# Two hybrid-attention blocks on one core: the second block's low weight parts on VectorE alone

## Chip, cores and metric

The kernel runs on one core of one Trainium2 chip. The metric is device time in microseconds, the median of several runs. A profile is one execution of the program, taken by the hardware profiler; times within it are microseconds from its first instruction (us), single instructions also nanoseconds (ns).

## What is computed

Two transformer blocks run one after the other on 256 tokens of width 1024, all in float32. The first ends in a mixture of 16,384 single-row experts. The change lies in the second block, which projects its normalised input with one large matrix `w_in` and feeds two mixers:

```python
def second_block(x, p, w_in, ...):
    u = rms_norm(h, norm_pre_mix[i])
    proj = u @ w_in[i]
    hq, hf, hi, hg, nq, nkv, ngate, ga, gb = jnp.split(proj, SPLIT_POINTS, axis=-1)
    kc, vc, ks, vs, kw, vw = jnp.split(nkv, 6, axis=-1)
    y_a = hgrn2_mixer(hq, hf, hi, hg, lower_bounds[i], hg_gnorm[i])
    y_b = nsa_mixer(nq, kc, vc, ks, vs, kw, vw, ngate, cmp_pe_k[i], cmp_pe_v[i], ...)
    merged = (jax.nn.sigmoid(ga) * (y_a @ w_branch_a[i])
              + jax.nn.sigmoid(gb) * (y_b @ w_branch_b[i]))
    h = h + rms_norm(merged @ w_out[i], norm_post_mix[i])
    ...
```

`nsa_mixer` is an attention of 16 query heads over 4 key groups with three branches: keys and values compressed from windows of 32 tokens by a small MLP, selected blocks (at 256 tokens, all of them), and a sliding window. Queries and keys are rotated (rope), and the branches are mixed by sigmoid gates. `hgrn2_mixer` is a gated linear recurrence that takes hq, hf, hi and hg.

## The kernel before, in words

**Split products.** Every weight matrix comes from HBM in blocks of 128x1024 floats, in a fixed list (`_plan`), through a ring of three buffers (w_raw), by DMAs of the SP queue. TensorE multiplies in a rounded format (fp32r), so each block is split: ScalarE writes the rounded part w_hi, and the low part w_lo = w_raw - w_hi is one subtraction of two 128x1024 operands. A product is three matmuls, w_hi by the activations' high part hh, w_lo by hh, w_hi by their low part hl (`mm3`). On PE, rows named ga are products with 512 columns (keys, values, queries, hi), rows named gc those with 256 (the gates' w2_ng, and hq and hf, one block per head).

**Who makes w_lo.** `low_part` (lines 366 to 378) chooses the engine when the program is written, by the planner's own estimates of when GpSimd (POOL) and VectorE (DVE) would be free:

```python
there = self.done["w", self.low][0] + HOP
by = lambda e, t: max(self.busy[e], there) + t
engine = self.nc.gpsimd if by("pool", 2.3) < by("dve", 1.14) + self.offload else self.nc.vector
```

`offload` is the last of four numbers that a stage sets: (depth, margin, backlog, offload). SIDE_A (line 30) holds from `nsa_in` on, for the second block's keys and values and the first half of the queries; SIDE_B (line 31) from the end of `nsa_in` on, for the compressed values, the products hq and hf, the second half of the queries, hi and the heads; SIDE_C (line 32) from `merge` on. The larger offload is, the more often POOL is chosen.

**The order of the work.** The order on PE, VectorE, ScalarE and SP is the order in which the Python code writes instructions. Main products are written in the plan's order. Between them `pump` writes steps of side generators (`turn` for keys and queries, `hidden`, `cmp_scores`, `cmp_values`, `head`) when, by the planner's estimates, what they need is ready ahead of PE, and stops when VectorE or ScalarE is booked more than `backlog` us ahead of PE. So where a low part is booked also moves side steps. A few places wait without choice (`until`): for R, the tokens' scale, for `flat`, the input of the compressing MLP, and for RT, R as a row.

**Names.** kvd, x2t: the keys and values to compress and their transposes. R, diag, RT: the scales, as a diagonal matrix and as a row. kr, krh, krl, krt: rotated keys, their two parts and transposes. qr, ro, qs, qst: queries, rope terms, their split parts and transposes. hid, hidk, hidv, kc, vc: the compressing MLP (weights cw1_k, cw1_v) and its second products. s, nm, nz, nP, nPt, no: a head's scores, negated maximum, normaliser, probabilities, their transposes and the product with the values. sc, pc, pct: the same of the compressed branch. zr, hq, hf: gate products scaled by RT and finished. The stage behind (`merge`) begins with the products hA of the recurrence, whose results are masked with lev, and the products of w2_hg; its constants npm, pmlp, gn and lev are loaded by DMAs of the POOL queue into space that the heads' tiles leave.

Of the kernel before, what the change touches and what calls it, by code (L numbers as in the profile page):

```python
# [26 lines left out]


SIDE_1 = 3, 0.4, 2.5, -9
SIDE_A = 4, 0.4, 2.5, 0  # L30
SIDE_B = 4, 0.3, 3.5, 2
SIDE_C = 4, 0.4, 6, -9
HOP = 0.18
E = mybir.EngineType
# [152 lines left out]
class Feed:  # L187
# [17 lines left out]
    def next(self):  # L205
        self.fetch()
        w = self.blocks[self.used]
        if self.timed:
            self.net.done[self.net.who()] = self.net.done["feed", self.used]
        self.used += 1  # L210
        return w
# [56 lines left out]
class Net:  # L268
# [1109 lines left out]
    def nsa_in(self, pool, lead):  # L1378
# [31 lines left out]
        self.gt = pool.tile([128, 2, 3, 16], F32, name="gt")  # L1410
        self.depth, self.margin, self.backlog, self.offload = SIDE_A

# [73 lines left out]
        def compress(k):  # L1486
            self.until(("flat", k))
            hp = self.acc("hid")[:, :256]
            for c4 in range(4):
                wh, wl = self.block("cw1_" + k, c4)  # L1490
                for s in range(4):
                    c = 4 * c4 + s
                    w = slice(s * 256, s * 256 + 256)
                    if c == 15:
                        nc.tensor.matmul(hp[:64], flat[k][:, c, 0], wl[:, w], start=False, stop=False)
                    nc.tensor.matmul(hp, flat[k][:, c].rearrange("p s m -> p (s m)"), wh[:, w], start=c == 0, stop=c == 15)
                    if c < 15:
                        nc.tensor.matmul(hp[:64], flat[k][:, c, 0], wl[:, w], start=False, stop=False)
                if c4 == 3:
                    self.late.append(lambda: self.side(hidden(k, hp), first=True))  # L1500
                yield
# [58 lines left out]
        self.queries(pool, 0, between=lambda: next(ck))  # L1560
        self.depth, self.margin, self.backlog, self.offload = SIDE_B
        return compress("v")
# [440 lines left out]
```

## Time and profile before

| | us |
|---|---|
| median of three runs (lowest, highest) | 1555.44 (1548.98, 1556.6) |
| the profiled execution's own time | 1553.87 |
| its span, first to last instruction | 1551.0 |
| PE busy in the span | 1363.1 (88%) |
| VectorE busy | 1036.8 (67%) |
| ScalarE busy | 714.8 (46%) |
| GpSimd busy | 395.7 (26%) |
| mean granted TensorE clock | 0.963 of full speed |

The first block with its gathered experts takes the first 898 us or so. The keys, queries and heads of the second block lie from about 905 to 1146.5 us, the recurrence and the merging products follow, and from about 1320 us on the MLP. Busy times overlap between engines; idle time of an engine costs only where others wait for it. A wait is put down to the work that ended it.

### The profile page before, as it was taken

How to read it: one execution, taken by the hardware profiler on the slowest of the kernel's cores; microseconds unless marked ns; L12 is line 12 of the kernel's file. 1: busy time of each engine (PE TensorE's matmuls, PEld its weight loads, DVE VectorE, ACT ScalarE, POOL GpSimd, SP SyncE). 2: the span in 40 equal slices, each digit the busy share in tenths (PEclk: the TensorE clock that was granted, in tenths of full speed). 3: DMA queues.
4: the chain of work that ended last, by engine and by line, in shares of the span. 5: the costliest groups of instructions: out<-in, count | busy, mean ns of one | idle time of the engine just before them, and what ended most of it. 6: DMA issues, size and time to landing. Idle time of an engine off the chain costs nothing.

```text
span 1551.0 us, 18352 instructions
## 1 busy us (share of the span) xinstructions
PE 1363.1 (88%) x5930; PEld 914.3 (59%) x5930; DVE 1036.8 (67%) x2175; ACT 714.8 (46%) x1668; POOL 395.7 (26%) x380
## 2 busy tenths in 40 slices
PE   7999988898878788778787889799999999999996
PEld 3778774444422233222222267778788887999875
DVE  5656767877676677666644567867648666876454
ACT  2434354554444444444433365455643654544443
POOL 2101044333333343333333222533330100000000
PEclk9989989999999999999999999899999999999998
DMA  8756639999999999999999845422254355656553
GB/s 341 249 156 226 193 123 418 421 421 422 421 422 422 421 421 422 421 421 421 421 422 420 342 130 170 142 86 69 82 164 123 111 185 167 185 186 182 189 164 107
DMA packets 81647, 418.99 MB, mean 270 GB/s; under 512 B 10288, under 2 KB 12752, under 8 KB 48656
## 3 DMA queue, kind: packets, MB, share of 16 engines
q0 software_dynamic: 42528, 288.17, 45.5%
q1 hardware_dynamic: 38736, 129.39, 26.1%
q8 instruction: 47, 0.77, 0.2%
q14 instruction: 48, 0.39, 0.1%
q10 hardware_dynamic: 288, 0.27, 0.0%
HBM read 416.75 MB, written 1.05 MB: 269 GB/s over the span
## 4 chain that ended last, share of the span: by engine, by line
PE 42%; DMA 34%; DVE 10%; issue 6%; ACT 3%; POOL 1%; SPq 0%; DVEq 0%; POOLq 0%; ACTq 0%
DMA uv<-in_uv,ids 32%; PE ga L224 19%; PE gc L224 10%; DVE junk L224 2%; PE va L224 2%; PE hA L224 2%; PE s L224 2%; PE wo L224 1%; PE no L224 1%; POOL uv L1164 1%; DVE w_lo L224 1%; PE nPt L224 1%; DMA w_ada<-in_ada 1%; PE o L224 1%; ACT w_hi L224 1%
## 5 line engine op out<-in xcount | busy, mean ns | idle before, releaser
L224 PE MATMUL va<-uv,diag 128*128 128x512 f32 x1024 | 506.9, 624 | 119.8 <-ACT diag L224 118.9
L224 DVE SCALAR_TENSOR_TENSOR junk<-uv,xr 128x1024 f32<-128x1024 f32 x256 | 311.9, 1218 | 203.0 <-DMA uv<-in_uv,ids 195.8
L224 PEld LDWEIGHTS va<-uv,diag 128*128 128x128 f32 x1024 | 179.5, 193 | 412.3 <-ACT diag L224 271.5
L1164 POOL DMA_INDIRECT uv<-in_uv,ids x256 | 247.9, 968 | 399.4 <-PE va L224 260.1
L224 ACT ACTIVATE w_hi<-w_raw 128x1024 fp32r<-128x1024 f32 x215 | 227.4, 1059 | 215.9 <-PE ga L224 139.6
L224 DVE TENSOR_TENSOR w_lo<-w_raw,w_hi 128x1024 fp32r<-128x1024 f32 x172 | 209.9, 1223 | 142.9 <-ACT w_hi L224 142.2
L224 ACT ACTIVATE ga<-dots 128x1 f32<-128x1 f32 x256 | 51.9, 203 | 347.8 <-DVE junk L224 346.6
L224 PE MATMUL gc<-hh,w_hi 128*128 128x256 f32 x520 | 170.6, 328 | 0.0
L224 PE MATMUL gc<-hl,w_hi 128*128 128x256 f32 x520 | 151.8, 292 | 1.4 <-DVE hl L224 1.4
L224 PE MATMUL gc<-hh,w_lo 128*128 128x256 f32 x520 | 151.6, 291 | 1.0 <-POOL w_lo L224 0.7
L224 POOL TENSOR_TENSOR w_lo<-w_raw,w_hi 128x1024 fp32r<-128x1024 f32 x43 | 103.5, 2413 | 169.6 <-ACT w_hi L224 162.4
L224 PEld LDWEIGHTS gc<-hl,w_hi 128*128 128x128 f32 x520 | 104.4, 201 | 11.5 <-issue 9.6
L224 PEld LDWEIGHTS gc<-hh,w_hi 128*128 128x128 f32 x520 | 104.5, 201 | 9.7 <-issue 9.6
L224 ACT ACTIVATE diag<-ident,c 128x128 f32<-128x128 f32 x256 | 102.8, 401 | 8.4
L224 PEld LDWEIGHTS gc<-hh,w_lo 128*128 128x128 f32 x520 | 104.1, 200 | 1.6 <-POOL w_lo L224 1.1
L224 PE MATMUL ga<-w_hi,hh 128*128 128x512 f32 x240 | 99.2, 413 | 0.4 <-ACT hh L224 0.2
L224 PE MATMUL ga<-w_lo,hh 128*128 128x512 f32 x240 | 94.5, 394 | 2.5 <-DVE w_lo L224 2.1
L224 PE MATMUL ga<-w_hi,hl 128*128 128x512 f32 x240 | 94.5, 394 | 0.4 <-DVE hl L224 0.4
L224 ACT ACTIVATE c<-ga,g 128x1 f32<-128x1 f32 x256 | 75.4, 294 | 8.3
L224 POOL TENSOR_TENSOR gr<-gv,nhalf 128x1 f32<-128x1 f32 x8 | 5.2, 656 | 287.8 <-DVE gv L224 287.8
L224 PEld LDWEIGHTS ga<-w_lo,hh 128*128 128x128 f32 x240 | 45.6, 190 | 11.5 <-DVE w_lo L224 3.1
L224 PEld LDWEIGHTS ga<-w_hi,hl 128*128 128x128 f32 x240 | 45.2, 188 | 11.2 <-DVE hl L224 1.3
(408 smaller groups left out, 2147.7 us busy)
## 6 DMA issues: line engine op xcount, KB each, us to landing
w_ada<-in_ada POOLq DMA_DIRECT2D x32, 512.0 KB, 4.7
w_raw<-in_w_up SPq DMA_DIRECT2D x32, 512.0 KB, 3.5
w_raw<-in_w_down SPq DMA_DIRECT2D x32, 512.0 KB, 3.5
ring<-in_ada SPq DMA_DIRECT2D x16, 512.0 KB, 9.6
w_raw<-in_wq SPq DMA_DIRECT2D x16, 512.0 KB, 6.2
w_raw<-in_w_kv SPq DMA_DIRECT2D x12, 512.0 KB, 4.7
w_raw<-in_w_out SPq DMA_DIRECT2D x8, 512.0 KB, 4.7
uv<-in_uv,ids POOLq DMA_INDIRECT x256, 17.7
```

Source lines behind the costliest of these rows:

```text
L224: r = call(out, *args, **kwargs)
L1164: tc.nc.gpsimd.indirect_dma_start(rows[i], None, I["uv"], bass.IndirectOffsetOnAxis(ap=ids[:, i % 16:i % 16 + 1], axis=0))
```

## The change

The offload of SIDE_A and of SIDE_B becomes -99, so that `low_part` never finds POOL earlier than VectorE while these two stages last. Nothing else is edited.

```diff
 SIDE_1 = 3, 0.4, 2.5, -9
-SIDE_A = 4, 0.4, 2.5, 0
-SIDE_B = 4, 0.3, 3.5, 2
+SIDE_A = 4, 0.4, 2.5, -99
+SIDE_B = 4, 0.3, 3.5, -99
 SIDE_C = 4, 0.4, 6, -9
```

In the recorded program 38 subtractions of 128x1024 move from POOL's queue to VectorE's. GpSimd's queue at the point where they stood (the rows named rstd are the small powers behind the norms, DMA rows load the constants of the stage behind):

```order
 L224 TENSOR_TENSOR rstd_6601<-ms_6599,nhalf 128x1
-L224 TENSOR_TENSOR w_lo<-w_raw,w_hi 128x1024
 L224 TENSOR_TENSOR rstd_6646<-ms_6644,nhalf 128x1
 L224 TENSOR_TENSOR rstd_6659<-ms_6657,nhalf 128x1
-L224 TENSOR_TENSOR w_lo<-w_raw,w_hi 128x1024 x35
 L224 DMA npm<-in_n_post_mix 128x1024
 L224 DMA pmlp<-in_n_pre_mlp 128x8
 L224 DMA gn<-in_gnorm 128x1
 L224 DMA lev<-in_lev 128x1024
-L224 TENSOR_TENSOR w_lo<-w_raw,w_hi 128x1024 x2
```

All 38 are gone there, and the four DMAs have nothing in front of them but rstd. VectorE at the beginning of the stage, where the keys to compress are scaled and R is made a diagonal:

```order
 L224 TENSOR_SCALAR Rh<-R 128x1
 L224 TENSOR_SCALAR kvd<-ga,R 128x1024
+L224 TENSOR_TENSOR w_lo<-w_raw,w_hi 128x1024
 L224 TENSOR_SCALAR diag<-ident,R 128x128 x2
 L224 TENSOR_TENSOR w_lo<-w_raw,w_hi 128x1024
 L224 COPY RT<-RT 128x128 x2
-L224 TENSOR_TENSOR w_lo<-w_raw,w_hi 128x1024
+L224 TENSOR_TENSOR w_lo<-w_raw,w_hi 128x1024 x2
```

One more low part stands between kvd and diag, one more behind RT. VectorE in the first gate products, where the MLP's hidk and the first query parts qs are made:

```order
 L224 TENSOR_TENSOR hidk<-hidk,hx 128x128
 L224 SCALAR_TENSOR_TENSOR hidk<-hidk,hx 128x128
+L224 TENSOR_TENSOR w_lo<-w_raw,w_hi 128x1024 x2
+L224 TENSOR_TENSOR zr<-gc,RT 128x256
+L224 TENSOR_SCALAR hidk<-hidk 128x128
+L224 TENSOR_TENSOR hidk<-hidk,hx 128x128
 L224 CAST qs<-qr 128x8x64
 L224 TENSOR_TENSOR qs<-qr,qs 128x8x64
-L224 TENSOR_TENSOR zr<-gc,RT 128x256
-L224 TENSOR_SCALAR hidk<-hidk 128x128
-L224 TENSOR_TENSOR hidk<-hidk,hx 128x128
```

Two low parts stand inside the MLP's chain now, and its end and a gate product come ahead of qs. On PE the side steps move against the main products as VectorE's bookings do: the last head's no products stood 54 ga matmuls ahead of the first hA, and now stand 18 ahead of it. The SP queue, and so the order of all weight loads, is the same.

## Rows read from the trace of the kernel before

**Rows 1.** By stage: length, busy time per engine (instructions), clock, DMA share, GB/s.
```profile
905.00:949.40 44.40, 38.03 (x186) 31.32 (x185) 32.07 (x56) 30.03 (x44) 12.25 (x8) 0.96 0.51 160
949.40:1011.00 61.60, 53.09 (x336) 48.16 (x335) 47.86 (x80) 30.85 (x50) 28.77 (x12) 0.89 0.52 155
1011.00:1057.00 46.00, 42.99 (x264) 34.89 (x264) 29.02 (x88) 28.49 (x91) 15.25 (x7) 0.93 0.25 80
1057.00:1101.00 44.00, 38.64 (x267) 34.30 (x266) 34.93 (x86) 22.32 (x65) 15.80 (x7) 0.88 0.24 75
1101.00:1146.50 45.50, 45.46 (x256) 36.54 (x255) 18.01 (x49) 28.44 (x71) 23.70 (x13) 1.00 0.44 137
1146.50:1242.00 95.50, 95.50 (x581) 84.53 (x580) 72.98 (x167) 42.35 (x85) 4.18 (x6) 1.00 0.39 121
```

**Rows 2.** What PE waited for, 905 to 1146.5: us in total, times, longest.
```profile
PE qst L224 <- DVE qs L224: 3.8, 2, 2.6
PE vc L224 <- issue: 3.0, 1, 3.0
PE nPt L224 <- DVE nP L224: 2.7, 2, 1.9
PE krt L224 <- DVE krh L224: 2.5, 2, 2.0
...
PE RT L224 <- DVE diag L224: 2.2, 1, 2.2
...
PE gc L224 <- POOL w_lo L224: 0.7, 2, 0.4
```

**Rows 3.** All engines in order of time: start, duration, operation [idle before <- what ended it].
```profile
980.72 4.76 POOL L224 TENSOR_TENSOR w_lo<-w_raw,w_hi 128x1024 fp32r<-128x1024 f32 x2 [2.96 <-ACT w_hi L224]
...
980.92 2.34 DVE L224 TENSOR_TENSOR hidk<-hidk,hx 128x128 f32<-128x128 f32 x1
...
983.36 1.09 PE L224 MATMUL kc<-hidk,w2k 128*128 128x64 f32 x4 [1.52 <-issue]
...
986.84 4.86 POOL L224 TENSOR_TENSOR w_lo<-w_raw,w_hi 128x1024 fp32r<-128x1024 f32 x2 [1.36 <-ACT w_hi L224]
...
989.53 2.71 DVE L224 TENSOR_TENSOR qs<-qr,qs 128x512 fp32r<-128x512 f32 x1
...
992.30 0.66 PE L224 MATMUL qst<-ident,qs 128*128 128x128 f32 x4 [2.62 <-DVE qs L224]
```

**Rows 4.** VectorE by tile: count, ns shortest/median/longest, first and last start.
```profile
L224 DVE TENSOR_TENSOR qs<-qr,qs x4: 693/693/2710, 979.7 to 1070.4; 128x512 fp32r<-128x512 f32 x4
...
L224 DVE SCALAR_TENSOR_TENSOR hq<-hq,zr x8: 411/1692/2427, 977.8 to 1103.8; 128x256 f32<-128x256 f32 x8
```

**Rows 5.** By shape, 905 to 1146.5: count | busy us, mean ns | idle before.
```profile
L224 DVE TENSOR_TENSOR w_lo<-w_raw,w_hi 128x1024 fp32r<-128x1024 f32 x15 | 18.3, 1222 | 30.1 <-ACT w_hi L224 29.7 <-PE krt L224 0.5
...
L224 POOL TENSOR_TENSOR w_lo<-w_raw,w_hi 128x1024 fp32r<-128x1024 f32 x38 | 91.4, 2411 | 139.4 <-ACT w_hi L224 132.3 <-PE s L224 3.8 <-PE nPt L224 3.3
```

**Rows 6.** By shape, the stage behind, 1146.5 to 1242.
```profile
L224 DVE TENSOR_TENSOR w_lo<-w_raw,w_hi 128x1024 fp32r<-128x1024 f32 x22 | 26.9, 1222 | 13.2 <-ACT w_hi L224 13.2
```

**Rows 7.** VectorE in order of time, first and last of 23 long entries.
```profile
913.67 1.60 DVE L224 TENSOR_TENSOR sc<-sc,rstd 128x1 f32<-128x1 f32 x2 [1.11 <-ACT junk L224]
...
1110.30 2.24 DVE L224 TENSOR_SCALAR hf<-hf,lcv,lbv 128x256 f32<-128x256 f32 x1 [0.43 <-ACT hf L224]
```

**Rows 8.** The chain that ended last, in order of time: start, duration, work.
```profile
1053.93 2.88 PE gc L224 x24
...
1134.13 12.47 PE ga L224 x54
```

**Rows 9.** In order of time: lev's DMA issue and its first reader.
```profile
1136.82 0.54 POOL L224 DMA_DIRECT2D lev<-in_lev  x1
...
1148.39 0.68 DVE L224 TENSOR_TENSOR A<-hA,lev 128x512 f32<-128x512 f32 x1
```

**Rows 10.** The tile lev: from issue to landing, us.
```profile
DMA to landing us min/median/max: 5.4/5.4/5.4
```

## Prediction, made before the result was known

> **What bounds the kernel now.** I read the stage table first [rows 1]: the stretch in which the second block makes its keys, values, queries and attention heads runs from 905.0 to 1146.5 us of the span, and TensorE is not full there. PE is busy for 218.2 of these 241.5 us (the sum of the first five lines), so it stands idle for 23.3 us, and its granted clock is 0.96, 0.89, 0.93, 0.88 and 1.00 in the five stretches: weighted with their lengths, (1 - clock) makes 1.8 + 6.8 + 3.2 + 5.3 = 17.1 us of full-speed work that was lost at the lower level, 1.2 instead of 2.4 GHz, after the gaps. In the next stage (line six) PE is busy for 95.5 of 95.5 us at clock 1.00. DMA is busy for about half of its time or less in all of them. So at most 23.3 + 17.1 = 40 us can be had here, and only if every gap goes.
>
> Next, what PE waits for [rows 2]. Six of its 13 rows stand there. The longest waits end on small VectorE results (qs, nP, krh, diag) that TensorE transposes or multiplies next; a low part made by POOL is waited for directly for only 0.7 us (the gc products). The wait of vc that is put down to "issue" is behind hidv, which is VectorE's too. So it is not the slow GpSimd subtraction that stops PE, but VectorE being late.
>
> Why it is late is in the timeline of both engines [rows 3]. POOL starts two low parts at 980.72 and two more at 986.84. The VectorE multiplication hidk, which starts at 980.92 behind the first of them, lasts 2.34 us and ends at 983.26, about when that one ends (half of 4.76 us); the subtraction of qs, at 989.53 beside the last of the four, takes 2.71 us. PE's product kc waits 1.52 us behind the first and its transposes qst 2.62 us for the second. The same shapes without POOL beside them are short [rows 4]: three of four qs subtractions take 693 ns, the fourth is this one with 2710; hq takes between 411 and 2427 ns. In the timeline of the stretch I find 23 entries that exceed their shape's shortest by over 0.5 us, from the one at 913.67 (two products of 128x1, 1.60 us together) to the one at 1110.30 [rows 7]; each lies beside a POOL subtraction for most of its length, and their excess adds up to 43 us. A VectorE instruction that reads two operands from SBUF, or copies or scales within it, stands still while POOL's w_lo runs.
>
> **The change part by part.** *What leaves POOL.* 38 subtractions of 2411 ns, 91.4 us of POOL [rows 5], which hardly anything else wants here. With them go the 43 us of standstill on VectorE.
>
> *What VectorE gets.* The same 38 at 1222 ns [rows 5], 46.4 us. VectorE's time in the stage goes from 161.9 us (the first five lines of [rows 1]) to 161.9 + 46.4 - 43.4 = 164.9 us: the load hardly moves. Against a stage of some 220 us this is 75%. The price of so loaded a VectorE is shown by the stage behind, where all 22 low parts are made by VectorE too [rows 6]: it is busy for 73.0 of 95.5 us, 76%, and PE has no gap. That is the nearest row, and I take it for the kind of load; the far end is that each moved subtraction waits at the head of VectorE's queue for its w_hi, which is a rival below.
>
> *What it does for latency.* A low part is there 1.22 instead of 2.41 us after its turn, so the waits for POOL itself go [rows 2]. The recorded order moves too, since the planner that writes it now books these subtractions to VectorE: most side steps (qst, s, nPt, no and what feeds them) stand 6 to 60 main products later on PE, the last no 36 later, so TensorE has more of its own work ahead of each.
>
> *What is left, stretch by stretch* (idle and clock loss, from [rows 1]):
> 1. 905.0 to 949.4, 6.4 + 1.8 = 8.2 us. The chain to R and diag loses its standstill at 913.67 [rows 7], but VectorE gets one low part in front of those sc products and one between kvd and diag, 2.4 us. I let PE's wait for diag (2.2 us) go down by half and the krh wait of 2.5 us go [rows 2], and with them half of the clock loss, since the lower level follows such a wait: a gain of 4.
> 2. 949.4 to 1011.0, 8.5 + 6.8 = 15.3 us, the densest in standstills, 21 of the 43 us. Here each product of hq or hf is followed by a cw1_v product, so two low parts are wanted in the time of 24 gc and 8 hid matmuls: 2.4 us of VectorE against 2.88 us [rows 8] and, at the same rate, 1.0 us. With qs, rope and hidk beside them VectorE is still about as long as PE in the first blocks, and I leave 5 us of loss: a gain of 10.
> 3. 1011.0 to 1057.0, 3.0 + 3.2 = 6.2 us, mostly the one wait for vc [rows 2]: a gain of 3.
> 4. 1057.0 to 1101.0, 5.4 + 5.3 = 10.7 us. Its waits are for nP, behind stretched instructions [rows 2]; the softmax chain keeps its own length, and a low part stands in it now and then: a gain of 6.
> 5. 1101.0 to 1146.5: PE is full, so nothing; VectorE is busy for 18.0 us here and has room for the heads that come later.
>
> *What it costs at the end of the stage.* The last head's no products now stand 18 instead of 54 ga products ahead of the next stage. 54 of them took 12.47 us [rows 8], so 36 are 8.3 us. POOL's four DMAs for that stage, the mask lev among them, waited until the heads were done: lev was issued at 1136.82, 5.4 us from issue to landing, so it was there at 1142.2, 6.2 us ahead of its first reader at 1148.39 [rows 9, 10]. Shifted by 8.3 us it comes up to 2 us late on VectorE. The hA products that follow have ga products beside them, so between 0 and 2 us; I take 1.
>
> *Sum.* 4 + 10 + 3 + 6 - 1 = 22 us. The profiled execution took 1553.9 us (span 1551.0), 1.6 us under the median of 1555.4; 1553.9 - 22 = 1532. If nothing of the 40 us is left, 1514, which I hold for out of reach, as some gaps are dependences that VectorE needs even at its own speed; with half of my gain, 1543.
>
> **The rivals.**
> *VectorE becomes the bound, slower than before.* VectorE works strictly in order, and a w_lo that waits for its w_hi holds back the softmax steps behind it. In this stage it already stood 30.1 us idle in front of its 15 low parts [rows 5], 2.0 us each. If the 38 new ones waited as long, 76 us would be added to 164.9 + 30, and 271 us exceeds the 241 of the stage: some 30 us slower, 1584. The point from which it decides is a wait of over 0.6 us each, since (218 - 195) / 38 = 0.6 keeps VectorE under PE's own time; below it the waits are covered. Half-way, at 1.5 us, 252 us would be 10 slower, 1564. For it: VectorE is the busiest engine but PE in the second stretch, 47.9 of 61.6 us [rows 1]. Against it: the 22 low parts of the next stage waited 13.2 us in all, 0.6 each, with PE full [rows 6]. The Trainium skill, "Perfetto Trace Analysis", section "Optimizing Scalar/DVE Operations", speaks for this rival, as it allows handing work from a saturated VectorE to GPSIMD; it adds that the two share an SBUF port, so that this might not help. By its first half the time would be this rival's, by its second the forecast's, and the standstills of [rows 3] agree with the second. Chance 0.12.
>
> *The gaps are latencies, no change.* If PE waits because chains like s, max, exp, reciprocal, scale, transpose are too long for the work that the order puts between them, a VectorE that is as loaded as before (164.9 against 161.9 us) gains only the direct waits of 0.7 us and some of the standstills: 2 to 6 us, 1548 to 1552. For it: busy time on VectorE does not fall. Against it: the waits of [rows 2] end on instructions that were themselves stretched, and the order puts more main products in between. Chance 0.14.
>
> *The change does not do what it says* can be put aside: no low part of this stage is left on POOL in the recorded order.
>
> **How the numbers follow.** The forecast (1532, from 1518 to 1545) has 0.74. A measurement of this kernel tells about 0.5% from no change, so faster means under 1547.7 us and slower over 1563.2. Faster 0.74, same 0.14, slower 0.12. Leaving out the slower rival and the lowest few per cent of the forecast, where nearly all of the loss would have to go, the range is 1520 to 1557.
>
> **What would show it.** VectorE's hq and hf near 0.41 us in every instance and no entry over 2 us but runs of several; its busy time in the stage near 165 us; 53 low parts on it at 1.22 us; PE's idle time there 6 to 12 instead of 23 us, and its clock at 0.95 or more; the stage some 220 us long. It is wrong if VectorE's instructions stay long without POOL beside them, if PE's waits move to w_lo or to ACT's w_hi, or if the hA products behind the stage begin to wait for lev.

## The result, and the profile after

| | before | after |
|---|---|---|
| median of six runs each, us | 1552.26 | 1527.52 |
| lowest to highest, us | 1548.98 to 1556.6 | 1523.23 to 1534.38 |
| span of the profiled execution, us | 1551.0 | 1527.7 |
| mean granted clock | 0.963 | 0.977 |
| VectorE / GpSimd busy in the span, us | 1036.8 / 395.7 | 1032.7 / 304.6 |

The ratio is 0.9845, 95% interval 0.9812 to 0.9878; measured again later it was 0.9899 (0.9877 to 0.9922). The two intervals hardly meet; faster by 1.0 to 1.6%.

In the profiled executions of this document the stage begins between 887.6 and 895.3 us, behind a first block that no edit touches, so kernels are compared by the stage itself, from the fill of kbd, GpSimd's first instruction of the stage, to the first hA product. It took 251.7 us before (894.7 to 1146.4) and takes 228.9 us after (892.9 to 1121.8): 22.8 us of the 23.3 us between the two spans. The tables below leave out its first 10.3 us, so that the table of before begins at 905.0 as in [rows 1].

The stage and 95.3 us behind it, after; columns as in [rows 1]: length, busy time (instructions) of PE, its weight loads, VectorE, ScalarE and GpSimd, clock, DMA share, GB/s.

```profile
903.20:1121.80 218.60, 204.14 (x1299) 172.70 (x1298) 156.44 (x393) 140.98 (x315) 4.45 (x8) 0.99 0.42 134
```
```profile
1121.75:1217.00 95.25, 93.89 (x574) 83.16 (x573) 72.04 (x170) 40.66 (x84) 4.86 (x7) 1.00 0.37 117
```

PE is idle for 14.5 us of the stage instead of 23.3, and its clock is 0.99 instead of 0.93. GpSimd has all but left. VectorE has 38 instructions more (393 for 355) and is busy for 5.5 us less than the 161.9 of [rows 1].

What PE waits for now, 905 to 1130 us; columns as in [rows 2]:

```profile
PE gc L224 <- DVE w_lo L224: 2.7, 3, 1.5
PE s L224 <- ACT nT L224: 2.4, 2, 1.9
PE krt L224 <- DVE krh L224: 2.1, 2, 1.5
PE nPt L224 <- ACT nP L224: 1.8, 1, 1.8
PE x2t L224 <- DVE kvd L224: 1.5, 2, 0.9
PE hA L224 <- DVE hq L224: 1.4, 1, 1.4
PE ga L224 <- DVE w_lo L224: 1.2, 1, 1.2
```

The waits for VectorE's qs, diag and nP and the wait of vc, which led [rows 2], are gone or under 1 us; the longest single one is 1.9 us. In their place stand 3.9 us for low parts and waits for ScalarE in the heads. The same tiles as in [rows 4], and the low parts as in [rows 5]:

```profile
L224 DVE SCALAR_TENSOR_TENSOR hq<-hq,zr x8: 414/422/426, 968.6 to 1070.2; 128x256 f32<-128x256 f32 x8
```
```profile
L224 DVE TENSOR_TENSOR qs<-qr,qs x4: 691/692/693, 974.2 to 1057.8; 128x512 fp32r<-128x512 f32 x4
```
```profile
L224 DVE TENSOR_TENSOR w_lo<-w_raw,w_hi 128x1024 fp32r<-128x1024 f32 x53 | 64.5, 1221 | 32.6 <-ACT w_hi L224 32.6
```

No instance is long any more: the eight hq lie between 414 and 426 ns, where the longest had 2427, and 53 low parts wait 32.6 us for ScalarE, 0.6 us each.

### The profile page after: what moved, and what is told of

It reads as the page before. It is cut to its first block, busy times and chain, and to the rows that moved or that the text cites. A ratio compares the mean times of both kernels' runs of the same rounds, so it can differ in the third digit from the quotient of the medians.

```text
span 1527.7 us, 18338 instructions
## 1 busy us (share of the span) xinstructions
PE 1342.5 (88%) x5930; PEld 895.8 (59%) x5930; DVE 1032.7 (68%) x2213; ACT 715.4 (47%) x1668; POOL 304.6 (20%) x342
## 4 chain that ended last, share of the span: by engine, by line
PE 36%; DMA 35%; DVE 11%; issue 8%; ACT 5%; POOL 1%; SPq 0%; DVEq 0%; POOLq 0%; ACTq 0%
DMA uv<-in_uv,ids 32%; PE ga L224 18%; PE gc L224 8%; PE va L224 3%; DVE junk L224 2%; DVE w_lo L224 2%; PE hA L224 2%; DMA w_ada<-in_ada 1%; ACT w_hi L224 1%; PE s L224 1%; PE no L224 1%; PE wo L224 1%; ACT diag L224 1%; ACT nP L224 1%; ACT L224 1%
## 5 line engine op out<-in xcount | busy, mean ns | idle before, releaser
L224 DVE TENSOR_TENSOR w_lo<-w_raw,w_hi 128x1024 fp32r<-128x1024 f32 x210 | 256.0, 1222 | 146.3 <-ACT w_hi L224 146.0
L224 PE MATMUL gc<-hh,w_hi 128*128 128x256 f32 x520 | 166.5, 320 | 0.0
L224 PEld LDWEIGHTS gc<-hl,w_hi 128*128 128x128 f32 x520 | 101.3, 195 | 11.3 <-issue 9.1
L224 PEld LDWEIGHTS gc<-hh,w_lo 128*128 128x128 f32 x520 | 101.0, 194 | 3.3 <-DVE w_lo L224 3.3
L224 PEld LDWEIGHTS ga<-w_hi,hh 128*128 128x128 f32 x240 | 45.7, 191 | 10.1 <-DVE vg L224 0.8
```

The costliest lines, as they stand in the source:

```text
L224: r = call(out, *args, **kwargs)
```

## Experiments

Three theories were to be told apart. *Standstill*: VectorE stands still while GpSimd subtracts, and PE waits for VectorE. *Order*: the gain comes from the side steps that the planner moved, because it books the low parts elsewhere. *Latency*: a low part is ready 1.2 us sooner. MOVED stands for the 38 blocks whose low part GpSimd made.

**The old order, with VectorE's low parts.** The planner decides and books as before, and only the instruction goes to the other queue. PE's order is then row for row that of the kernel before.

```diff
+        if self.low in MOVED and engine is self.nc.gpsimd:
+            self.tc.nc.vector.tensor_tensor(wl, w, wh.bitcast(F32), op=ALU.subtract)
+            self.count("pool", 0.08 + 1024 / 500)
+        else:
```

> The order of the kernel before, with the planner still booking the 38 low parts to GpSimd, but each issued to VectorE at the place in the program where it stood. Standstill theory (VectorE stands still while GpSimd subtracts): nearly all of the gain is here, 1525 to 1537 us, no VectorE entry over 2 us but long shapes, VectorE busy near 165 us in the stage, PE idle there 10 to 18 us. Order theory (the gain comes from the side steps that the planner moved): as before, 1548 to 1556 us. Latency theory (a low part is there 1.2 us sooner): also faster, but then the next kernel of this list must be slower only by direct waits for w_lo.

Measured: 1531.16 us, ratio 0.9895 (0.9861 to 0.9928). The stage takes 229.4 us, PE is idle for 14.2 us, VectorE busy for 156.6:

```profile
897.90:1117.00 219.10, 204.90 (x1298) 173.83 (x1297) 156.59 (x393) 140.34 (x315) 4.48 (x8) 0.98 0.43 136
```
```profile
L224 DVE SCALAR_TENSOR_TENSOR hq<-hq,zr x8: 415/418/424, 964.6 to 1074.3; 128x256 f32<-128x256 f32 x8
```

The stage is within 0.5 us of the changed kernel's. The new order is not needed for the gain. To be sure, both were run again on one chip:

> The changed kernel itself, on the same chip as the three others here. All theories: 1524 to 1532 us.

> The old order with the low parts on VectorE again, beside the changed kernel on one chip. The stages differed by 0.5 us in the profiles. If the new order is worth nothing: within 3 us of the line above. If it is worth something: 3 to 8 us slower than that line.

Measured: the changed kernel 1531.38 us, ratio 0.9899 (0.9877 to 0.9922), stage 230.2 us; the old order 1530.64 us, 0.9898 (0.9877 to 0.9920), stage 229.5 us. What the planner moved is worth nothing that shows. With the low parts on VectorE, the order theory has fallen.

**The new order, with GpSimd's low parts.** The reverse: the changed kernel's order, the same 38 subtractions issued to GpSimd.

```diff
+        if self.low in MOVED:
+            self.tc.nc.gpsimd.tensor_tensor(wl, w, wh.bitcast(F32), op=ALU.subtract)
+            self.count("dve", 0.07 + 1024 / 960)
+        else:
```

> The order of the changed kernel, with the planner booking to VectorE, but the same 38 low parts issued to GpSimd. Standstill theory: the standstills come back (hq and hf up to 2.4 us, some 40 us of excess on VectorE), 1543 to 1556 us, a little under the kernel before at best since its order leaves more main products ahead of the side steps. Order theory: 1525 to 1532 us. Latency theory: PE and its weight loads wait directly for GpSimd's w_lo by 15 us or more, VectorE's short shapes stay short, 1540 to 1550 us.

Measured: 1564.49 us, ratio 1.0111 (1.0075 to 1.0148), slower than before and slower than any theory had it. The stage takes 260.6 us:

```profile
899.70:1150.00 250.30, 218.00 (x1298) 183.31 (x1297) 166.91 (x355) 140.79 (x315) 96.38 (x46) 0.94 0.38 117
```
```profile
PE nPt L224 <- DVE nP L224: 13.8, 7, 3.5
...
PE hid L224 <- POOL w_lo L375: 2.4, 1, 2.4
...
PE gc L224 <- POOL w_lo L375: 1.7, 2, 1.0
...
PE ga L224 <- POOL w_lo L375: 0.9, 2, 0.6
```
```profile
L224 DVE TENSOR_SCALAR hf<-hf,lcv,lbv x8: 402/1335/2299, 986.1 to 1102.3; 128x256 f32<-128x256 f32 x8
```

The long instances are back, and PE waits for nP, not for low parts: 5.0 us for POOL against 13.8 for nP. In the kernel before it waited for POOL's low parts for 1.1 us, the 0.7 us of [rows 2] and this:

```profile
PE ga L224 <- POOL w_lo L224: 0.4, 1, 0.4
```

So the latency of the low part looks like a small term; no run has late low parts without standstills, so its share is read from these waits. Nor do the weights come sooner after the change: over the stage ScalarE waits for loads for 7.5 us before and 8.7 us after. That this kernel is 9 us worse than the old order with the same standstills is not settled. All of it is idle time of PE (250.3 - 218.0 = 32.3 us, against 23.3); the order was written with shorter VectorE steps than it then meets, but so was the old one.

**GpSimd load alone.** The changed kernel, with 38 subtractions more on GpSimd that nobody reads.

```diff
         engine.tensor_tensor(wl, w, wh.bitcast(F32), op=ALU.subtract)
+        if self.low in MOVED:
+            scr = self.nsa.tile([128, 1024], F32, name="scr", tag="scr", bufs=1)
+            self.tc.nc.gpsimd.tensor_tensor(scr, w, wh.bitcast(F32), op=ALU.subtract)
```

> The changed kernel, with 38 subtractions of the same shape and operands on GpSimd besides, whose results nothing reads (added work, nothing left out). Standstill theory: VectorE has all low parts and the standstills too, some 165 + 40 to 55 = 205 to 220 us busy in the stage, and is the bound: 1550 to 1585 us, slower than the kernel before or like it. Order and latency theories: both are untouched, 1525 to 1532 us.

Measured: 1596.95 us, ratio 1.0322 (1.0282 to 1.0361); the stage takes 293.3 us:

```profile
902.60:1185.60 283.00, 224.95 (x1299) 186.98 (x1298) 221.25 (x393) 141.23 (x315) 111.98 (x46) 0.90 0.33 103
```
```profile
PE nPt L224 <- DVE nP L224: 17.4, 8, 3.9
PE gc L224 <- DVE w_lo L224: 13.2, 4, 6.6
PE ga L224 <- DVE w_lo L224: 6.4, 4, 3.1
```

VectorE makes the same 393 instructions and is busy for 221.25 instead of 156.44 us: 64.8 us of standstill, from work whose results no engine uses. The stage is 64 us longer, and the time 12 us above the range of the standstill theory. Not all of that need be standstill: the added subtractions read w_raw and w_hi, so the buffers of the ring come free later, and the queue of the weight loads waits for them:

```profile
SPq L351 <- POOL scr L377: 35.5, 16, 2.2
```

ScalarE waits for loads for 17.0 us in this stage, against 8.7 us in the changed kernel. How much of the 64 us that is was not separated; VectorE's busy time shows the standstill alone.

**GpSimd that only writes.** The same place and number, but two fills of the tile instead of the subtraction, with a VectorE fill of one column ahead to keep them in place.

```diff
-            self.tc.nc.gpsimd.tensor_tensor(scr, w, wh.bitcast(F32), op=ALU.subtract)
+            self.tc.nc.vector.memset(scr[:, :1], 0.0)
+            self.tc.nc.gpsimd.memset(scr, 0.0)
+            self.tc.nc.gpsimd.memset(scr, 1.0)
```

> The changed kernel with added GpSimd work as in the third kernel, but two fills of a 128x1024 tile for each of the 38 low parts (writes only, no operand is read; a VectorE fill of one column in front keeps their place in time). If what VectorE stands still for is GpSimd's reading of SBUF: products of two SBUF operands (hq, nz, qs) stay short, and only forms that copy or scale within SBUF (hf, nP, qs cast) may be held; 1527 to 1545 us. If any GpSimd instruction holds VectorE: as the third kernel, hq up to 2.4 us, 1560 to 1600 us. If it is GpSimd's load on something shared by all (order of issue, semaphores): PE waits grow without long VectorE entries.

Measured: 1539.19 us, ratio 0.9941 (0.9915 to 0.9968), stage 238.9 us. GpSimd is busy for 77.8 us in it, and VectorE for 170.1:

```profile
L224 DVE SCALAR_TENSOR_TENSOR hq<-hq,zr x8: 414/422/426, 967.4 to 1075.3; 128x256 f32<-128x256 f32 x8
```
```profile
L224 DVE TENSOR_SCALAR hf<-hf,lcv,lbv x8: 405/658/1254, 977.3 to 1081.9; 128x256 f32<-128x256 f32 x8
```
```profile
L224 DVE CAST qs<-qr x4: 415/495/969, 973.6 to 1061.5; 128x512 fp32r<-128x512 f32 x4
L224 DVE TENSOR_TENSOR qs<-qr,qs x4: 691/692/693, 974.7 to 1061.9; 128x512 fp32r<-128x512 f32 x4
```

Products of two SBUF operands (hq, the qs subtraction) are not held by a fill, though five of the eight hq and two of the four qs lay beside one; forms that copy or scale one operand within SBUF (hf, the qs cast) are, for up to one fill of 966 ns. So the two kinds of VectorE instruction are not held by the same GpSimd work. The fills read no weight buffer and leave low parts and order as they are: the 13.7 us more of VectorE (2.2 of them the small fills in its own queue) come with 10.0 us more of stage.

**One number alone.**

```diff
-SIDE_B = 4, 0.3, 3.5, 2
+SIDE_B = 4, 0.3, 3.5, -99
```

> Only the second number is changed (SIDE_B, 33 of the 38 low parts: compressed values, hq, hf, second queries, hi, heads). Standstill theory: 38.8 of the 43.4 us of standstill lie in this part, so 1528 to 1535 us, within 5 us of the whole change. If the first part (SIDE_A, keys and first queries, 5 low parts) carries more than its share: 1537 to 1546 us.

Measured: 1536.37 us, ratio 0.9909 (0.9880 to 0.9938), stage 234.5 us: 17.2 of the 22.8 us, from 33 of the 38. The time lies between the two ranges that were expected.

```diff
-SIDE_A = 4, 0.4, 2.5, 0
+SIDE_A = 4, 0.4, 2.5, -99
```

> Only the first number is changed (SIDE_A, keys and first queries, 5 of the 38 low parts). Standstill theory: 4.6 of the 43.4 us of standstill go, 1546 to 1551 us, with what the second number alone leaves out (about 5 us of stage length) at most. If the two parts help each other, less than 3 us.

Measured: 1544.27 us, ratio 0.9969 (0.9947 to 0.9991), stage 246.8 us, 4.9 us shorter; the time is 2 us under the expected range. 17.2 + 4.9 = 22.1: the parts add up, and five low parts at the start of the stage, where keys wait for R and for rope, carry a fifth of the gain.

**The mask for the stage behind, loaded early.** After the change VectorE and then PE wait for lev at the joint of the stages; in order of time, changed kernel:

```profile
1119.94 0.56 POOL L224 DMA_DIRECT2D lev<-in_lev  x1
...
1125.41 0.69 DVE L224 TENSOR_TENSOR A<-hA,lev 128x512 f32<-128x512 f32 x1 [5.19 <-DMA lev<-in_lev]
...
1126.85 1.08 PE L224 MATMUL hA<-hq,k 128*128 128x64 f32 x8 [1.36 <-DVE hq L224]
```
```diff
-            lev = pool.tile([128, 8, 128], U32, name="lev")
-            nc.gpsimd.dma_start(lev, I["lev"])
+            lev = self.lev    # loaded at the beginning of second()
```

> The changed kernel with the mask lev loaded at the beginning of the second block into a space of its own. In the changed kernel the first masked product waited 5.2 us for it and PE 1.4 us. If that is the late load alone: the PE wait in front of the second hA products goes, the stage behind is 1.0 to 1.5 us shorter, the time 1526 us within its scatter. If the wait has another cause behind it (w_lo in front of the second masked product): PE still waits 0.5 us or more there.

Measured: 1528.82 us, one run. The 95.3 us behind the stage are without a gap again:

```profile
1122.50:1217.80 95.30, 95.30 (x581) 84.47 (x580) 73.35 (x172) 41.66 (x84) 5.04 (x8) 1.00 0.37 116
```

So the late load was the cause of that gap. 1.4 us are below what the runs can tell.

**More room in the planner.** With lev early, the margin of both stages at 0.8 us:

```diff
-SIDE_A = 4, 0.4, 2.5, -99
-SIDE_B = 4, 0.3, 3.5, -99
+SIDE_A = 4, 0.8, 2.5, -99
+SIDE_B = 4, 0.8, 3.5, -99
```

> The kernel of the line above (lev early) with the planner's margin at 0.8 us in both stages instead of 0.4 and 0.3, so that side steps are written later against PE's main products. If what is left of PE's waits in the stage (14.5 us) is VectorE and ScalarE being some tenths late: half of it goes, 1518 to 1523 us. If it is the low parts waiting for the loads and ScalarE: no change, 1524 to 1529 us. If the side steps then pile up at the end: slower than 1530 us.

Measured: 1555.82 us, ratio 1.0042 (1.0027 to 1.0058), the whole gain given back. By stretch:

```profile
1003.00:1050.00 47.00, 46.45 (x340) 41.12 (x339) 34.68 (x88) 29.91 (x88) 0.00 (x0) 1.00 0.44 135
...
1100.00:1120.00 20.00, 9.81 (x42) 6.57 (x42) 5.93 (x21) 6.00 (x21) 0.00 (x0) 0.68 0.00 0
1120.00:1149.80 29.80, 19.54 (x83) 13.87 (x84) 7.34 (x23) 10.74 (x29) 1.71 (x3) 0.70 0.07 20
```

PE is nearly full from 1003 to 1050, as hoped, but the heads that were put off pile up: between 1100 and 1120 nothing is loaded (DMA share 0.00), the next weight load is issued at 1148.27, and PE goes from head to head, waiting 22.8 us in nine times for nP, with the clock at 0.7.

More heads in work at a time should cure that: depth 6, backlog 6, and margin 0.5 in the heads' stage, then 0.6 in both.

```diff
-SIDE_B = 4, 0.3, 3.5, -99
+SIDE_B = 6, 0.5, 6, -99
```

> The changed kernel with lev loaded early and the planner's stage for the heads at depth 6, margin 0.5, backlog 6 (from 4, 0.3, 3.5): more heads are in work at a time, so each step can be written later behind its input and the last no still stands well ahead of the end of hi (90 main products instead of 18). If what is left is VectorE and ScalarE being some tenths late at the side steps: PE idle in the stage 6 to 10 us instead of 14.5, 1519 to 1525 us. If the low parts' own waits are what is left: 1525 to 1530 us.

> As the line above, with margin 0.6 in both stages (the keys' stage had 0.4). The keys' waits (krt, x2t, 3.6 us) go down by 1 to 2 us if they are lateness of tenths; they stay if they are the forced waits for R and k. 1517 to 1525 us, within 3 us of the line above.

Measured: 1533.86 us (ratio 0.9912, 0.9890 to 0.9933) and 1531.34 us (0.9892, 0.9864 to 0.9920), stages of 236.6 and 234.0 us, both slower than any range that was expected; beside them the changed kernel had 1531.38 us and 230.2 us. PE's idle time, 17.4 and 17.0 us, did not fall; in the second it waits most for ScalarE's nP:

```profile
PE s L224 <- ACT nP L224: 6.0, 5, 2.8
PE gc L224 <- DVE w_lo L224: 3.2, 3, 1.6
```

No version was found that is faster than the changed kernel by more than the runs can tell.

## Why the prediction was right

- **The mechanism** was as forecast. VectorE's long instances were standstills: they vanish with GpSimd's subtractions in either order, and return with GpSimd load whose results nothing reads.
- **VectorE's time** was forecast at 165 us and is 156.4. Two terms were mis-sized. Without its low parts VectorE is busy for 144.4 us before and 97.2 after, so the standstill is 47.2 us, not the 43.4 that I got from entries with over 0.5 us of excess. And the 38 low parts added 59.1 - 17.4 = 41.7 us, not 46.4, since the records of consecutive VectorE instructions overlap. Moving the low parts relieved VectorE by 5.5 us. That is much less than the 22.8 us of stage: the standstills lay in instructions that PE waited for [rows 2, 3], while PE waits for low parts for only 3.9 us after the change. This is read from the waits. It fits the two kernels with added GpSimd work, where 64.8 and 13.7 us more of VectorE came with 64 and 10 us more of stage.
- **The rate of a moved low part**, 1.22 us, and its wait for w_hi held: 32.6 us for 53, 0.6 us each, as in the stage behind [rows 6]. The slower rival's point of 0.6 us was meant for the 38 new ones on top of the 30.1 us of the old 15, some 53 us in all, so it was not near.
- **By stretch.** Since the old order with VectorE's low parts has the same instructions on PE as before, its stretches can be compared one by one, at the gate products that stand next to the limits of [rows 1]. The starts of these products are counted from the fill of kbd in each kernel, and a stretch's gain is what its end came earlier by, less what its beginning did.

| stretch of [rows 1] | forecast gain, us | measured, old order with VectorE |
|---|---|---|
| 1, to the gates' product | 4 | 3.1 |
| 2, to the first product of the fourth head's hq | 10 | 12.2 |
| 3, to the first of the fifth head's hf | 3 | -0.1 |
| 4, to the first of the last head's hf | 6 | 8.3 |
| 5, to hA | 0 | -1.2 |

The sum, 22.3, is the forecast's 23 within a us, but the third stretch gained nothing (the wait for vc only fell from 3.0 to 1.5 us, and others came), and the second and fourth, where clock and standstills were worst, gained more.
- **Idle time and clock.** The step that failed in its split: I looked for PE idle 6 to 12 us and a clock of 0.95 or more, and it is 14.5 us and 0.99. Gaps gave 23.3 - 14.5 = 8.8 us; PE's busy time for the same 1299 instructions fell from 218.2 to 204.1 us, 14.1 us, which goes with the clock: it stood at 1.2 GHz in six places of the stage before, some 34 us in all, and in one place, for some 3 us, after. The longest wait went from 3.0 to 1.9 us.
- **The joint with the next stage.** Forecast 0 to 2 us, 1 taken: PE waits 1.4 us, by the mechanism that was named, and early loading removes it.
- **The order** was given as a help ("more of its own work ahead of each"). With the low parts on VectorE it is worth nothing that shows.
- **The rivals.** Under the latencies rival there would have been 2 to 6 us; the standstills of [rows 3] were in those chains. The saturation rival's wait did not come: VectorE stood idle before its low parts for 32.6 us, against 30.1 before [rows 5]. The kernel with GpSimd load comes nearest to it: VectorE is busy for 221 us, more than the 205 that PE needs in the changed kernel, PE waits 19.6 us for low parts, and the stage takes 293. But there it is the standstills that fill VectorE, not waits for w_hi. The Trainium skill, "Perfetto Trace Analysis", section "Optimizing Scalar/DVE Operations", allows an offload from a saturated VectorE and warns of the shared port in the same breath. Here the warning decides, by 47.2 us of standstill for 41.7 us of work taken off.

The total was forecast at 1532 us and is 1527.5; against the profiled execution of before 22 us were forecast, and the stage with its joint gave 22.8 - 1.4 = 21.4. The two profiled executions differ by 24.3 us; of the rest 1.8 us are an earlier start of the stage, and about 1 us lies outside the span.

That the sum agrees within a us is partly luck. The kernel before was profiled once, with a granted clock of 0.963; 36 later executions of it had 0.963 to 0.974 and medians of 1551.14, 1550.39 and 1548.03 us. Beside them the gain was 16.7 us for the changed kernel and 17.4 and 20.0 us for the old order with VectorE's low parts, so 22.8 us of stage may be some us more than usual.

## What to carry to other kernels

Before an elementwise step is handed from VectorE to GpSimd, look at VectorE's own durations in the stretch: if the same shape takes 0.4 us in one place and 2.4 in another, and the long ones end with a GpSimd instruction, the offload may cost VectorE more than it saves, and it shows as busy time, not as waiting. Count that excess against the work that the move would bring back (here 47.2 against 41.7 us), and look at which of the two the slowest engine waits for. And test a suspected collision by adding idle load of the same kind to the faster kernel, with a second one that holds none of the kernel's buffers.

## What the hardware showed that was not expected

Which VectorE instructions are held depends on both sides. Beside GpSimd subtractions, which read SBUF, two-operand products as well as copies and scalings are held, while VectorE products with one operand in PSUM are not. In the kernel before, two of the 17 zr products lay wholly beside subtractions, in the kernel with the idle load five, and all took between 408 and 426 ns. First one of before, then the kernel with the idle load:

```profile
1055.98 2.39 POOL L224 TENSOR_TENSOR w_lo<-w_raw,w_hi 128x1024 fp32r<-128x1024 f32 x1 [5.63 <-ACT w_hi L224]
...
1056.85 0.42 DVE L224 TENSOR_TENSOR zr<-gc,RT 128x256 f32<-128x256 f32 x1 [1.26 <-PE gc L224]
```
```profile
L224 DVE TENSOR_TENSOR zr<-gc,RT x17: 408/416/425, 951.7 to 1131.1; 128x256 f32<-128x256 f32 x17
```

Beside GpSimd fills, which read nothing, two-operand products run free, and only copies and scalings are held. The Trainium skill, "SBUF — State Buffer", section "Who interferes with whom", has this rule: two SBUF inputs collide with a GpSimd instruction that reads SBUF, and the forms that use both ports for one operand collide with any. The runs agree in all four cases.

The same number of subtractions held VectorE for longer in the kernel with the idle load: 64.8 us, against 47.2 us in the kernel before. Some 6 us of it fall on the low parts themselves, which took 1338 ns in the mean instead of 1221. GpSimd is slowed too there: its subtractions took 2830 ns in the mean, against 2411 [rows 5]. That VectorE has more to do in that kernel is a likely reason for both, but no run shows it.
